# Four start addresses for the low weight buffers, one for all moving operands, and two instruction orders, in a one-core encoder kernel

## Chip, core and metric

The kernel runs on one core of a Trainium2 chip. The metric is the device time of one execution in microseconds (us); the table below gives the median of three runs. Each core has a matrix engine (PE, with its weight loads shown apart as PEld), a vector engine (DVE), a scalar engine (ACT), a general engine (POOL) and a queue that issues most transfers (SP).

## What is computed

Two layers over 272 tokens (16 learned meta tokens ahead of 256 others) of width 1024. Each layer is a parallel pair of token mixers (a chunked two-way retention with 8 heads, and a windowed attention with a sink) followed by an MLP with a squared ReLU. Cut to what matters:

```
h = concat([meta_tokens, x])                       # 272 x 1024
for l in range(2):
    u = rms_norm(h, norm_mix_pre[l])
    q_r, k_r, v_r, g_r, q_a, k_a, v_a, gate_r, gate_a = split(u @ w_in[l])
    y_r = retention_branch(q_r, k_r, v_r, g_r, log_decay) @ w_ret_o[l]
    y_a = attention_branch(q_a, k_a, v_a, attn_sink[l]) @ w_att_o[l]
    mix = (sigmoid(gate_r) * y_r + sigmoid(gate_a) * y_a) @ w_mix_o[l]
    h = h + rms_norm(mix, norm_mix_post[l])
    u = rms_norm(h, norm_ff_pre[l])
    h = h + rms_norm(square(relu(u @ w_ff1[l])) @ w_ff2[l], norm_ff_post[l])
return h[16:]
```

All of it is float32.

## The kernel before

**Products in three parts.** Each weight matrix is cut into units, 128 x 1024 numbers each, 130 per layer. A unit is fetched by one transfer into a `raw` buffer. ACT copies it, rounded, into a `wh` buffer (line 131), and DVE writes what the rounding lost, `raw - wh`, into a `wl` buffer (line 132). The tokens are split in the same way (`uh` and `ul`, `rh` and `rl`, `zh` and `zl`, `fh` and `fl`, two halves of `ao`). A product is then three matmuls, in `mm3`: high weights with high tokens (line 136), high weights with low tokens (line 137), low weights with high tokens (line 138). The weights are the stationary operand, which PE loads beforehand (PEld), 128 columns at a time; the tokens are the moving operand, 272 columns in layer 0, and 256 in most of layer 1, where the meta tokens are no longer needed (`c0 = 16`). A unit is eight such triples, 24 matmuls. The load for line 138, from `wl`, runs while line 137 streams; the loads for lines 136 and 137, both from `wh`, run while lines 138 and 136 stream. The last product of layer 1, `ff2t`, is turned round: the tokens (`fh`, `fl`) are stationary and 512 columns of `wh` or `wl` move (lines 848 to 850, 12 matmuls a unit).

**Where the buffers begin.** What matters here is the address of an operand within a partition, modulo 256 bytes; it is called its phase below. `raw`, `wh` and `wl` have rings of three, four and four buffers; unit i uses buffer i modulo 4, so DVE may be four units ahead of PE. All four `wh` and all four `wl` buffers begin at phase 0, and so does each 128-column piece of them (512 bytes). The slots of the tokens begin at phase 64, set by a small unused tile ("gap"), and a row of tokens is 320 numbers, 1280 bytes, so each row has the same phase. `tokens(..., at=n)` puts the tokens n columns into the row. With `at=32` the moving operand is at phase 192; in layer 1 `at=16` and `c0 = 16` give the same. So nearly all moving operands are at 192. The exceptions are `rl`, `zh` and `zl` of layer 0, at 0 (`at=48`); the 14 units of layer 1 that still need all 272 tokens, at 128; and in layer 1's MLP, the stationary `fh` and `fl`, at 64 (`at=48`), with `wh` and `wl` moving at 0.

**What sets the order.** A scheduler of the language orders the instructions of each engine; `tc.issue_after(x)` holds what is written in its block behind x. Each engine runs its own list in order. Three places are touched. In `value_r`, DVE scales a value head into `vt` (line 424), POOL copies its 16 meta tokens four times into `pads` (line 427, named `mine` in the code), and `centre()` gives PE one matmul from `pads` (line 430) and then two from `vt` (line 432), which show as two records each. In the retention, `meta(t)` forms scores of the meta tokens: PE (line 661), DVE `tmx` out of a bank of `ps_s` (through the helper of line 93), ACT `tm` (line 663), DVE `tm` (line 664). `similar` and `retained` are a head's scores (PE lines 680 and 681, DVE `sd`) and outputs (PE line 691 from `sd`, line 692 from `tm`). `ps_s` has two banks. At head 0, eight DVE steps `gt<-tg` add the tanh `tg` (ACT, line 647) to the gates `gt`.

Of the kernel before, what the change touches and what calls it, by code (L numbers as in the profile page):

```python
# [10 lines left out]
F32R = mybir.dt.float32r  # L11
# [6 lines left out]
P = 128  # L18
D = 1024
# [22 lines left out]
def encoder(ctx: ExitStack, tc: tile.TileContext, order, w, h_in, gains, dec, decm, sink, sinkm, tabs, mats, esel, masks, rel, relm, grow, out):  # L42
# [46 lines left out]
    def f(t):  # L89
        return t.bitcast(F32)  # L90

    def stt(o, a, s, b, op0=mul, op1=mul):
        V.scalar_tensor_tensor(out=o, in0=a, scalar=s, in1=b, op0=op0, op1=op1)
# [14 lines left out]
    def fetch(parts=1):  # L108
# [6 lines left out]
        for c in cuts:  # L115
            nc.sync.dma_start(raw[:, c], w[i][:, c])
            yield

    def unit(*name):
        i = len(order)  # L120
        order.append(name)
        if not raws:
            list(fetch())
        raw, cuts = raws.pop(0)
        wh = ring.tile([P, D], F32R, tag="wh", name="wh")
        wl = ring.tile([P, D], F32R, tag="wl", name="wl")
        for c in cuts:
            with ExitStack() as later:
                for ins in held.get(i, ()):
                    later.enter_context(tc.issue_after(ins))  # L130
                A.activation(wh[:, c], raw[:, c], AF.Copy)  # L131
                V.tensor_tensor(out=wl[:, c], in0=raw[:, c], in1=f(wh[:, c]), op=sub)  # L132
        return wh, wl
# [117 lines left out]
    def lead():  # L251
        x = [tokens(i, "u" + "hl"[i]) for i in range(2)]
        s8 = slot(7, "s8")
        ss = one.tile([P, T], F32, tag="ss", name="ss")
        ps = [bank("asas"[m], [T]) for m in range(4)]
        behind = {}

        def put(e, method, *args, **kw):
            if e in behind:
                with tc.issue_after(behind[e]):  # L260
                    ins = method(*args, **kw)
            else:
                ins = method(*args, **kw)
            behind[e] = ins.ins

        def squares(j):
            put("A", A.activation, s8[:, 2 * j:2 * j + 2], h[:, 2 * j:2 * j + 2], AF.Square)

        def add_squares(j):
            put("V", V.scalar_tensor_tensor, out=s8[:, 0:2], in0=s8[:, 0:2], scalar=4e-6 if j == 1 else 0.0, in1=s8[:, 2 * j:2 * j + 2], op0=add, op1=add)  # L270

        for k in range(KD):
            j, c = k // 2, slice(k % 2 * 512, k % 2 * 512 + 512)
            if k % 2 == 0:
                order.append(("lead", j))
                wh = ring.tile([P, D], F32R, tag="wh", name="wh")
                wl = ring.tile([P, D], F32R, tag="wl", name="wl")
            gk = g[:, 0, 0, k:k + 1]
            put("A", A.activation, wh[:, c], leads[j][:, c], AF.Copy)
            put("A", A.activation, x[0][:, k], h[:, k], AF.Copy, scale=gk)  # L280
            put("V", V.scalar_tensor_tensor, out=x[1][:, k], in0=h[:, k], scalar=gk, in1=f(x[0][:, k]), op0=mul, op1=sub)
            put("V", V.tensor_tensor, out=wl[:, c], in0=leads[j][:, c], in1=f(wh[:, c]), op=sub)
            if k in (3, 5, 7):
                squares((k - 3) // 2)
            if k in (6, 7):
                add_squares(k - 5)
            for m in range(4):
                o = k % 2 * 512 + m * P
                mm3(ps[m], wh[:, o:o + P], wl[:, o:o + P], x[0][:, k], x[1][:, k], k == 0, k == KD - 1)
        squares(3)  # L290
        add_squares(3)
        put("V", V.tensor_tensor, out=ss, in0=s8[:, 0], in1=s8[:, 1], op=add)
        held[len(order)] = [behind["V"]]
        return x, ss, ps
# [68 lines left out]
    for l in range(DEPTH):  # L363
# [52 lines left out]
        def value_r(hh):  # L416
            q, m = hh // 4, hh % 4
            if m == 0:
                tpv[q] = bank("s", [4, P]), [bank("t") for _ in range(2)]
            tpm, tps = tpv[q]  # L420
            vt = ready.get(hh)
            if vt is None:
                vt = two.tile([P, T], F32, tag="t1", name="vt")
                last = V.scalar_tensor_tensor(out=vt, in0=early.pop(0) if early else proj(u, 0, "a", "v_r", hh), scalar=-0.5, in1=rb, op0=mul, op1=mul)
                scaled.append(last.ins)
            mine = vtm[:, m]
            G.tensor_copy(mine[:, :, 16 * (m % 2):16 * (m % 2) + 16], fourfold(vt[:, 0:16]))

            def centre():
                PE.matmul(tpm[:, m], mine, mat["cen"], start=True, stop=True)  # L430
                for c in range(2):
                    PE.matmul(tps[c][:, m * P:(m + 1) * P], vt[:, 16 + c * P:16 + (c + 1) * P], mat["cen"], start=True, stop=True)
                if m == 3:
                    for c in range(2):
                        A.activation(vr[:, c, q * 512:(q + 1) * 512], tps[c], AF.Copy)
                    A.activation(vm[:, 4 * q:4 * q + 4], tpm, AF.Copy)
                    for r in odds:
                        low = vm[r, 4 * q:4 * q + 4]
                        V.tensor_tensor(out=low, in0=tpm[r], in1=f(low), op=sub)

            deferred.append(centre)
            if early:
                flush()
# [208 lines left out]
        def meta(t):  # L652
# [8 lines left out]
                PE.matmul(ps[:, c0:], kblk[min(i, 2)][:, t], q[:, c0:], start=i == 0, stop=i == 3)  # L661
            stt(x[:, c0:], ps[:, c0:], 0.125, x[:, c0:])
            A.activation(tm[:, t, c0:], x[:, c0:], AF.Copy)
            V.tensor_tensor(out=tm[lows, t, c0:], in0=x[lows, c0:], in1=f(tm[lows, t, c0:]), op=sub)

        sds, pos, pvs = {}, {}, {}

# [40 lines left out]
        similar(0)  # L708
        fill(F[3])
        with behind():  # L710
            meta(0)
        fill(F[4])
        for hh in range(8):
            with behind():
                if hh < 7:
                    similar(hh + 1)
                retained(hh)
            fill(F[7])
            if hh == 0:
                for m in range(KD):  # L720
                    stt(gt[:, m, c0:], tg[:, m, c0:], 1.0, gt[:, m, c0:], op0=add)
                rh, rl = tokens(7, "rh", at=32 - c0), tokens(8, "rl", at=(48, 16)[l])
            if hh % 2 and hh < 7:
                with behind():
                    meta((hh + 1) // 2)
            fill(F[6])
            with behind():
                last = normed(hh)
            fill(F[5])
# [16 lines left out]
                    mm3(ps[:, c0:], wh[:, sl], wl[:, sl], ao[:, 0, k, c0:], ao[:, 1, k, c0:], k == 0, k == 3)  # L746
                stt(tha[m][:, c0:], tha[m][:, c0:], 1.0, ps[:, c0:], op0=add)

        z = tokens(2, "zh", at=(48, 16)[l]), tokens(3, "zl", at=(48, 16)[l])
        for m in range(KD):  # L750
            ps = proj((rh, rl), c0, wide(), "ret_o", m)
            stt(thr[:, m, c0:], thr[:, m, c0:], 1.0, ps[:, c0:], op0=add)
# [25 lines left out]
        for m in range(KF):  # L778
            if m % KD == 0:
                a, b = ((5, 7), (8, 9), (6, 10), (2, 3))[m // KD]  # L780
                at = (32, 48)[l]
                low = [tokens(i, "fl", (4,), at) for i in ("10a", "10b")] if b == 10 else [tokens(b, "fl", at=at)]
                fs.append((rows(tokens(a, "fh", at=at)), sum(map(rows, low), [])))
            ps = proj(u, c0, wide(), "ff1", m)
            if l == 0 and 0 <= m - SUM < KD:
                accumulate(m - SUM)
# [201 lines left out]
```

## Time and profile before

| | |
|---|---|
| median of 3 runs | 874.17 us (872.90 to 877.86) |
| the profiled execution's own time | 876.77 us |
| its span, first to last instruction | 875.0 us |
| PE busy, PEld busy | 855.7 us (98%), 821.0 us (94%) |
| DVE, ACT, POOL busy | 604.0 us (69%), 558.1 us (64%), 55.4 us (6%) |
| DMA | 142 MB, mean 162 GB/s |

Times in the profile count from the first instruction of the span. A record of a matmul runs from its start to its modelled end and overlaps the next one, so its length is not what it costs; what it costs is the distance from its start to the start of the next. Where two rows of a timeline and the number of matmuls from one to the other are known, that distance is the difference over the number. A longer record goes with a longer distance: 276 ns with 113 ns, 281 ns with 118 ns.

### The profile page before, as it was taken

What the parts mean: (1) busy time and instruction counts of PE and PEld (TensorE: products, weight loads), DVE (VectorE), ACT (ScalarE), POOL (GpSimd) and SP (SyncE); (2) the same over time, 40 slices, a digit from 0 to 9 for tenths busy, and PEclk for the clock granted to TensorE, in tenths of its full rate; (3) what the DMA queues carried; (4) which work ended last, traced back from release to release, by engine and by line L of the source; (5) the groups of instructions that cost most, each with busy time, mean ns of one, the idle gap of its engine ahead of it and who ended that gap; (6) DMA issues with size and microseconds to landing.
All of it is one profiled execution on the core that took longest, in us unless ns stands there. A gap on an engine that the chain in (4) does not pass through costs nothing.

```text
span 875.0 us, 16673 instructions
## 1 busy us (share of the span) xinstructions
PE 855.7 (98%) x6514; PEld 821.0 (94%) x6514; DVE 604.0 (69%) x1113; ACT 558.1 (64%) x1034; POOL 55.4 (6%) x113
## 2 busy tenths in 40 slices
PE   9999999999999999999999999999999999999997
PEld 9899999999989999999989999999999999998885
DVE  7789788777768655544469898888686666554443
ACT  7447887666557877544355588976755588773432
POOL 2123320000000000000000032200000000000000
PEclk9999999999999999999999999999999999999999
DMA  8444444355645656656544535444366376656661
GB/s 300 161 142 123 122 143 129 118 166 157 179 147 163 197 171 177 184 171 183 178 121 145 155 119 162 143 148 121 121 199 205 104 216 210 195 199 192 181 187 67
DMA packets 41407, 142.15 MB, mean 162 GB/s; under 512 B 5360, under 2 KB 6256, under 8 KB 41328
## 3 DMA queue, kind: packets, MB, share of 16 engines
q1 hardware_dynamic: 40896, 140.43, 52.3%
q8 instruction: 51, 0.84, 0.4%
q10 hardware_dynamic: 432, 0.66, 0.2%
q14 instruction: 28, 0.23, 0.1%
HBM read 140.02 MB, written 1.05 MB: 161 GB/s over the span
## 4 chain that ended last, share of the span: by engine, by line
PE 79%; DVE 10%; ACT 7%; issue 2%; DMA 1%; POOL 0%; SPq 0%; DVEq 0%; ACTq 0%; POOLq 0%
PE ps_a L137 12%; PE ps_a L136 12%; PE ps_a L138 12%; PE ps_s L138 5%; PE ps_s L137 5%; PE ps_s L136 5%; PE ps_t L136 4%; PE ps_t L137 4%; PE ps_t L138 4%; DVE wl L132 3%; PE ps_a L850 2%; PE ps_s L850 2%; PE ps_s L848 2%; PE ps_a L848 2%; PE ps_a L849 2%
## 5 line engine op out<-in xcount | busy, mean ns | idle before, releaser
L132 DVE TENSOR_TENSOR wl<-raw,wh 128x1024 fp32r<-128x1024 f32 x256 | 312.7, 1224 | 204.9 <-ACT wh L131 203.1
L131 ACT ACTIVATE wh<-raw 128x1024 fp32r<-128x1024 f32 x256 | 270.0, 1058 | 205.4 <-PE ps_a L137 59.2
L136 PE MATMUL ps_a<-uh,wh 128*128 128x272 f32 (+1 forms) x912 | 265.6, 291 | 2.8 <-ACT uh L242 2.8
L137 PE MATMUL ps_a<-ul,wh 128*128 128x272 f32 (+1 forms) x912 | 259.5, 285 | 0.0
L138 PE MATMUL ps_a<-uh,wl 128*128 128x272 f32 (+1 forms) x912 | 259.2, 284 | 0.2 <-DVE wl L132 0.2
L136 PEld LDWEIGHTS ps_a<-uh,wh 128*128 128x128 f32 x912 | 172.4, 189 | 4.5 <-ACT uh L242 3.2
L137 PEld LDWEIGHTS ps_a<-ul,wh 128*128 128x128 f32 x912 | 172.5, 189 | 1.0
L138 PEld LDWEIGHTS ps_a<-uh,wl 128*128 128x128 f32 x912 | 172.2, 189 | 0.7 <-DVE wl L132 0.6
L138 PE MATMUL ps_s<-uh,wl 128*128 128x272 f32 (+1 forms) x184 | 52.1, 283 | 0.3 <-DVE wl L132 0.3
L136 PE MATMUL ps_s<-uh,wh 128*128 128x272 f32 (+1 forms) x184 | 52.1, 284 | 0.0
L137 PE MATMUL ps_s<-ul,wh 128*128 128x272 f32 (+1 forms) x184 | 52.1, 283 | 0.0
L136 PE MATMUL ps_t<-uh,wh 128*128 128x272 f32 (+1 forms) x152 | 43.2, 284 | 1.3 <-ACT uh L242 1.3
L137 PE MATMUL ps_t<-ul,wh 128*128 128x272 f32 (+1 forms) x152 | 43.1, 284 | 0.0
L138 PE MATMUL ps_t<-uh,wl 128*128 128x272 f32 (+1 forms) x152 | 42.8, 282 | 0.0
L138 PEld LDWEIGHTS ps_s<-uh,wl 128*128 128x128 f32 x184 | 34.6, 188 | 0.5 <-DVE wl L132 0.5
L136 PEld LDWEIGHTS ps_s<-uh,wh 128*128 128x128 f32 x184 | 34.9, 190 | 0.0
L137 PEld LDWEIGHTS ps_s<-ul,wh 128*128 128x128 f32 x184 | 34.8, 189 | 0.0
L136 PEld LDWEIGHTS ps_t<-uh,wh 128*128 128x128 f32 x152 | 28.6, 188 | 1.5 <-ACT uh L242 1.5
L137 PEld LDWEIGHTS ps_t<-ul,wh 128*128 128x128 f32 x152 | 28.6, 188 | 0.1
L138 PEld LDWEIGHTS ps_t<-uh,wl 128*128 128x128 f32 x152 | 28.6, 188 | 0.0
L97 DVE TENSOR_TENSOR fl<-ft,fh 128x272 fp32r<-128x272 f32 (+1 forms) x64 | 27.6, 433 | 1.0 <-ACT fh L96 0.9
L96 ACT ACTIVATE fh<-ft 128x272 fp32r<-128x272 f32 (+1 forms) x64 | 27.1, 424 | 1.7
(308 smaller groups left out, 1959.1 us busy)
## 6 DMA issues: line engine op xcount, KB each, us to landing
raw<-in_w SPq DMA_DIRECT2D x256, 512.0 KB, 3.6
leads<-in_w SPq DMA_DIRECT2D x6, 256.0 KB, 5.4
tab<-in_tabs SPq DMA_DIRECT2D x2, 544.0 KB, 6.1
h<-in_h_in SPq DMA_DIRECT2D x3, 272.0 KB, 5.4
out<-yt SPq DMA_DIRECT2D x3, 256.0 KB, 2.1
leads<-in_w ACTq DMA_DIRECT2D x2, 256.0 KB, 3.6
gj<-in_grow SPq DMA_DIRECT2D x1, 512.0 KB, 4.6
mats<-in_mats SPq DMA_DIRECT2D x1, 320.0 KB, 7.3
```

Source lines behind the costliest of these rows:

```text
L96: A.activation(xh, x, AF.Copy)
L97: V.tensor_tensor(out=xl, in0=x, in1=f(xh), op=sub)
L131: A.activation(wh[:, c], raw[:, c], AF.Copy)
L132: V.tensor_tensor(out=wl[:, c], in0=raw[:, c], in1=f(wh[:, c]), op=sub)
L136: PE.matmul(ps, ah, bh, start=first, stop=False)
L137: PE.matmul(ps, ah, bl, start=False, stop=False)
L138: return PE.matmul(ps, al, bh, start=False, stop=last)
L848: PE.matmul(pss[i], xh, wh[:, sl], start=kk == 0, stop=False)
L849: PE.matmul(pss[i], xh, wl[:, sl], start=False, stop=False)
L850: PE.matmul(pss[i], xl, wh[:, sl], start=False, stop=kk == KF - 1)
```

## The change

The four `wl` buffers get tags of their own and 16 more columns each (64 bytes), so that they begin at phases 0, 64, 128 and 192; unit i uses buffer i modulo 4 as before. Every `at` becomes `32 - c0`: the moving `rl`, `zh` and `zl` of layer 0 go from phase 0 to 192, and the stationary `fh` and `fl` of layer 1 from 64 to 192. Two orders are turned: in `centre()` the matmul from `pads` comes last; and the eight `gt<-tg` steps are held behind the last step of `meta(0)`.

```
+    def low_part(i):
+        return ring.tile([P, D + 16], F32R, tag=f"wl{i % 4}", name="wl", bufs=1)[:, :D]
...
-        wl = ring.tile([P, D], F32R, tag="wl", name="wl")
+        wl = low_part(i)
...
             def centre():
-                PE.matmul(tpm[:, m], mine, mat["cen"], start=True, stop=True)
                 for c in range(2):
                     PE.matmul(tps[c][:, m * P:(m + 1) * P], vt[:, 16 + c * P:16 + (c + 1) * P], mat["cen"], start=True, stop=True)
+                PE.matmul(tpm[:, m], mine, mat["cen"], start=True, stop=True)
...
-            V.tensor_tensor(out=tm[lows, t, c0:], in0=x[lows, c0:], in1=f(tm[lows, t, c0:]), op=sub)
+            return V.tensor_tensor(out=tm[lows, t, c0:], in0=x[lows, c0:], in1=f(tm[lows, t, c0:]), op=sub)
...
         with behind():
-            meta(0)
+            ready = meta(0)
...
                 for m in range(KD):
-                    stt(gt[:, m, c0:], tg[:, m, c0:], 1.0, gt[:, m, c0:], op0=add)
-                rh, rl = tokens(7, "rh", at=32 - c0), tokens(8, "rl", at=(48, 16)[l])
+                    with tc.issue_after(ready.ins):
+                        stt(gt[:, m, c0:], tg[:, m, c0:], 1.0, gt[:, m, c0:], op0=add)
+                rh, rl = tokens(7, "rh", at=32 - c0), tokens(8, "rl", at=32 - c0)
...
-        z = tokens(2, "zh", at=(48, 16)[l]), tokens(3, "zl", at=(48, 16)[l])
+        z = tokens(2, "zh", at=32 - c0), tokens(3, "zl", at=32 - c0)
...
-                at = (32, 48)[l]
-                low = [tokens(i, "fl", (4,), at) for i in ("10a", "10b")] if b == 10 else [tokens(b, "fl", at=at)]
-                fs.append((rows(tokens(a, "fh", at=at)), sum(map(rows, low), [])))
+                low = [tokens(i, "fl", (4,), 32 - c0) for i in ("10a", "10b")] if b == 10 else [tokens(b, "fl", at=32 - c0)]
+                fs.append((rows(tokens(a, "fh", at=32 - c0)), sum(map(rows, low), [])))
```

The scheduler answers to the two turned orders in the attention and retention stretches of both layers; outside them each engine's list is the same. Three places follow, first before, then after. After the change, line numbers below 116 are the same, later ones are 3 to 5 higher.

PE, in layer 0, where two value heads are centred at once, between the first matmuls of a unit. Before:

```order
L136 MATMUL ps_a<-uh,wh 128x272
L137 MATMUL ps_a<-ul,wh 128x272
L432 MATMUL ps_t<-mats,vt 128x128
L430 MATMUL ps_s<-mats,pads 128x128
L432 MATMUL ps_t<-mats,vt 128x128
L430 MATMUL ps_s<-mats,pads 128x128
L432 MATMUL ps_t<-mats,vt 128x128 x2
L138 MATMUL ps_a<-uh,wl 128x272
```

After:

```order
L139 MATMUL ps_a<-uh,wh 128x272
L140 MATMUL ps_a<-ul,wh 128x272
L434 MATMUL ps_t<-mats,vt 128x128 x2
L435 MATMUL ps_s<-mats,pads 128x128
L434 MATMUL ps_t<-mats,vt 128x128 x2
L435 MATMUL ps_s<-mats,pads 128x128
L141 MATMUL ps_a<-uh,wl 128x272
```

Each matmul from `pads` now stands behind both matmuls from its `vt`.

DVE, in layer 0, at the first attention keys and queries (`t` are temporaries of the rotation, `kal` the low part of the keys, `qa` the queries). Before:

```order
L451 TENSOR_TENSOR kal<-t_462,ka 64x272
L392 TENSOR_TENSOR t_510<-t_509,t_510 128x272
L451 TENSOR_TENSOR kal<-t_462,ka 64x272
L132 TENSOR_TENSOR wl<-raw,wh 128x1024
L93 SCALAR_TENSOR_TENSOR qa<-t_510,qa 64x272 x2
L424 SCALAR_TENSOR_TENSOR vt<-ps_a,rb 128x272
L132 TENSOR_TENSOR wl<-raw,wh 128x1024
```

After:

```order
L454 TENSOR_TENSOR kal<-t_462,ka 64x272
L394 TENSOR_TENSOR t_509<-ps_a,tab 128x272
L135 TENSOR_TENSOR wl<-raw,wh 128x1024
L454 TENSOR_TENSOR kal<-t_462,ka 64x272
L395 TENSOR_TENSOR t_510<-t_509,t_510 128x272
L427 SCALAR_TENSOR_TENSOR vt<-ps_a,rb 128x272
L135 TENSOR_TENSOR wl<-raw,wh 128x1024
L93 SCALAR_TENSOR_TENSOR qa<-t_510,qa 64x272 x2
```

The step that makes `vt` now stands ahead of the two `qa` steps, which stood ahead of it.

DVE, in layer 1, at the start of the retention. Before:

```order
L93 SCALAR_TENSOR_TENSOR sd<-ps_s,tt 128x256 x2
L93 SCALAR_TENSOR_TENSOR gt<-tg,gt 128x256 x5
L93 SCALAR_TENSOR_TENSOR tmx<-ps_s,tmx 128x256
L93 SCALAR_TENSOR_TENSOR gt<-tg,gt 128x256
L93 SCALAR_TENSOR_TENSOR thr<-ps_a,rb 128x256
L93 SCALAR_TENSOR_TENSOR sd<-ps_s,tt 128x256 x2
L664 TENSOR_TENSOR tm<-tmx,tm 64x256
L93 SCALAR_TENSOR_TENSOR gt<-tg,gt 128x256 x2
```

After:

```order
L93 SCALAR_TENSOR_TENSOR sd<-ps_s,tt 128x256 x2
L93 SCALAR_TENSOR_TENSOR tmx<-ps_s,tmx 128x256
L678 TENSOR_TENSOR tt<-tt,tb 128x128
L93 SCALAR_TENSOR_TENSOR thr<-ps_a,rb 128x256
L667 TENSOR_TENSOR tm<-tmx,tm 64x256
L93 SCALAR_TENSOR_TENSOR sd<-ps_s,tt 128x256 x2
L93 SCALAR_TENSOR_TENSOR gt<-tg,gt 128x256 x8
L135 TENSOR_TENSOR wl<-raw,wh 128x1024
```

`tmx` no longer stands behind five of the `gt` steps; all eight now stand in one block behind `tm`, with a `wl` step behind them. On PE the matmul from `tm` (line 692 before) moves from behind five matmuls of a unit to directly behind the two from `sd`.

## Rows read from the trace of the kernel before

**Rows 1.** The page: busy time, granted clock in 40 slices, chain by engine.

```profile
PE 855.7 (98%) x6514; PEld 821.0 (94%) x6514; DVE 604.0 (69%) x1113; ACT 558.1 (64%) x1034; POOL 55.4 (6%) x113
PEclk9999999999999999999999999999999999999999
PE 79%; DVE 10%; ACT 7%; issue 2%; DMA 1%; POOL 0%; SPq 0%; DVEq 0%; ACTq 0%; POOLq 0%
```

**Rows 2.** Timeline of PE, layer 0, `ff1`: start, length, instruction; 264 matmuls apart.

```profile
316.12 0.29 PE L136 MATMUL ps_a<-uh,wh 128*128 128x272 f32 x1
...
348.68 0.29 PE L136 MATMUL ps_s<-uh,wh 128*128 128x272 f32 x1
```

**Rows 3.** Timeline of PE, layer 0: `ret_o` (168 apart), then `mix` (120 apart).

```profile
205.85 0.28 PE L136 MATMUL ps_a<-rh,wh 128*128 128x272 f32 x1
...
226.75 0.29 PE L136 MATMUL ps_a<-rh,wh 128*128 128x272 f32 x1
...
235.76 0.29 PE L136 MATMUL ps_t<-zh,wh 128*128 128x272 f32 x1
...
250.80 0.29 PE L136 MATMUL ps_t<-zh,wh 128*128 128x272 f32 x1
```

**Rows 4.** Timeline of PE, layer 1: `ret_o` (192 apart), then `ff1` (624 apart).

```profile
638.88 0.28 PE L136 MATMUL ps_t<-rh,wh 128*128 128x256 f32 x1
...
661.49 0.28 PE L136 MATMUL ps_a<-zh,wh 128*128 128x256 f32 x1
...
700.81 0.28 PE L136 MATMUL ps_a<-uh,wh 128*128 128x256 f32 x1
...
771.53 0.28 PE L136 MATMUL ps_a<-uh,wh 128*128 128x256 f32 x1
```

**Rows 5.** Timeline of PE, layer 1, `ff2t`: 300 matmuls apart.

```profile
784.32 0.39 PE L848 MATMUL ps_s<-wh,fh 128*128 128x512 f32 x1
...
854.32 0.39 PE L848 MATMUL ps_s<-wh,fh 128*128 128x512 f32 x1
```

**Rows 6.** Groups of PE at 157.45, 172.34 and 142.55 us: count, busy us, mean ns.

```profile
L138 PE MATMUL ps_a<-uh,wl 128*128 128x272 f32 x1 | 0.3, 285 | 0.0
...
L138 PE MATMUL ps_a<-uh,wl 128*128 128x272 f32 x1 | 0.3, 292 | 0.0
...
L138 PE MATMUL ps_a<-uh,wl 128*128 128x272 f32 x1 | 0.3, 288 | 0.0
```

**Rows 7.** The same at 600.30 and 614.16 us, layer 1.

```profile
L138 PE MATMUL ps_a<-uh,wl 128*128 128x256 f32 x1 | 0.3, 276 | 0.0
...
L138 PE MATMUL ps_a<-uh,wl 128*128 128x256 f32 x1 | 0.3, 278 | 0.0
```

**Rows 8.** Timeline of PE in layer 0, with idle time before and what ended it.

```profile
28.59 0.49 PE L430 MATMUL ps_s<-mats,pads 128*128 128x128 f32 x2 [0.66 <-POOL pads L427]
...
43.60 0.49 PE L432 MATMUL ps_t<-mats,vt 128*128 128x128 f32 x2 [1.32 <-DVE vt L424]
44.82 0.80 PE L430 MATMUL ps_s<-mats,pads 128*128 128x128 f32 x2 [0.74 <-POOL pads L427]
```

**Rows 9.** Timeline of POOL and of DVE around the first of these.

```profile
27.37 1.17 POOL L427 COPY pads<-vt 128x64 f32<-128x64 f32 x1 [0.21 <-DVE vt L424]
...
27.23 1.22 DVE L132 TENSOR_TENSOR wl<-raw,wh 128x1024 fp32r<-128x1024 f32 x1
```

**Rows 10.** Timeline of DVE, ACT and PE in layer 1, start of the retention.

```profile
570.52 1.77 DVE L93 SCALAR_TENSOR_TENSOR gt<-tg,gt 128x256 f32<-128x256 f32 x5 [0.94 <-ACT tg L647]
...
575.32 2.35 DVE L132 TENSOR_TENSOR wl<-raw,wh 128x1024 fp32r<-128x1024 f32 x2
...
572.22 0.40 ACT L673 ACTIVATE tt<-rel,de 128x144 f32<-128x144 f16 x1
...
572.68 0.39 PE L680 MATMUL ps_s<-qk,qkl 128*128 128x256 f32 x1 [1.17 <-DVE tmx L93]
...
581.74 0.28 PE L138 MATMUL ps_a<-uh,wl 128*128 128x256 f32 x1
```

More of the change, by code (lines that the diff above doesn't have):

```diff
@@ L276, in lead @@
                 wh = ring.tile([P, D], F32R, tag="wh", name="wh")
-                wl = ring.tile([P, D], F32R, tag="wl", name="wl")
+                wl = low_part(j)
             gk = g[:, 0, 0, k:k + 1]
```

## The prediction, made before the changed kernel had run

> **What bounds the kernel now.** I read the page first: PE is busy for 98% of the span, PE makes up 79% of the chain that ended last, DVE 10% and ACT 7%, and the granted clock is at its upper level, 2.4 GHz, in all 40 slices [rows 1]. So a change pays or costs mainly through the distance from one matmul's start to the next. This I take from the timeline. In layer 0's `ff1`, 264 matmuls of 272 columns take 32.56 us, 123.33 ns each [rows 2]; 272 cycles of 2.4 GHz would be 113.3 ns, so some 10 ns of each is something else. Nothing waits there, and only addresses differ between this stretch and others of the same shape. `mix` of layer 0, all of whose moving operands are at phase 0, takes 15.04 us for 120, 125.33 ns; `ret_o` of layer 0, where only `rl` is at 0, 20.90 us for 168, 124.40 ns [rows 3]. Phases therefore matter, by a nanosecond or three. In layer 1, 256 columns take 113.33 ns in `ff1` (70.72 us for 624) but 117.76 ns in `ret_o` (22.61 us for 192), with the same phases, moving at 192 and weights at 0 [rows 4]: there are two rhythms at this width, and the trace does not say what picks one. `ff2t` takes 70.00 us for 300, 233.33 ns [rows 5].
>
> **The low weights' phases.** What changes is the load from `wl`, which runs while line 137 streams: 1824 of the 5472 loads for `mm3`. Of them 1040 are in layer 0 (130 units of 8), 672 in the 256-column units of layer 1, and 112 in its 272-column units, whose moving operand is at 128. A quarter of the buffers stays at phase 0. For the other phases the retention gives a price, because the key blocks that PE loads behind line 138 step through all four phases from head pair to head pair (a key row is 1088 bytes, 64 modulo 256). The last matmul of a unit ahead of such a load, moving at 192, has a record of 285 ns when the key is at 0, 292 ns when at 64, 288 ns when at 192 [rows 6], and the row at 128 reads the same as the last. Against the first that is 0, 7, 3 and 3 ns, 3.25 on average. In a stretch without interruption records swing by about 3 ns from one matmul to the next, and 285 is the low one, so against the mean of the swing it is 0, 5.5, 1.5 and 1.5, or 2.1. I take 2.5. `ret_o` supports a net cost of this size: there one matmul of three has moving and stationary operand at the same phase, as buffer 3 will have, and a triple takes 3 x 1.07 = 3.2 ns more than in `ff1` [rows 2, 3]. Layer 0: 1040 x 2.5 ns = 2.6 us. At 256 columns the record reads 276 ns at phase 0 and 278 ns at 64 [rows 7]; I let the other two cost nothing: 672 x 2 ns / 4 = 0.3 us. The 112 triples with a moving operand at 128 I leave at 0. **Sum +2.9 us**, on the path, since nothing covers PE. Upper end: 7 ns for three buffers of four in all triples, 1824 x 5.25 ns = 9.6 us. Lower end: no row shows a phase that is faster than 0, but layer 1's best rhythm is 113.33 / 256 = 0.443 ns a column, at which 272 would take 120.4; 2.9 ns off 780 loads is -2.3 us.
>
> The Trainium skill speaks against any price here: "SBUF — State Buffer", section "Who interferes with whom", gives PE two independent read ports, one for the moving operand and one for the weight loads, and says that PE never waits on anyone. By it this term would be 0. The records of 285 and 292 ns with the same moving operand and different weights [rows 6] disagree, as far as single matmuls can, and so do the 125.33 ns of `mix` [rows 3].
>
> **The moving operands.** `mix` of layer 0 goes from 125.33 to 123.33 ns (192 matmuls, 0.38 us) and `ret_o` from 124.40 to 123.33 (192, 0.21 us): **-0.6 us** [rows 2, 3]. In `ff2t` the stationary tokens go from 64 to 192, so that the moving `wh` stands 64 ahead of them instead of 192, and `wl` anything from 0 to 192. No row has 512 columns with another distance. The nearest is the distance of 64 at 272 columns (key at 128 under 192), +3 ns in its record; with the same 2.5 ns for all 384 matmuls I take **+1.0 us**. Ends: 7 ns, +2.7 us, and the rate of 0.443 ns a column, 226.7 instead of 233.33 ns, -2.5 us.
>
> **The turned orders.** (a) At 28.59 us PE waits 0.66 us for the copy to `pads` [rows 8]. That copy takes 1.17 us beside a `wl` step of 1.22 us that starts 0.14 us ahead of it [rows 9]. After the change that `wl` step stands behind another `vt` step and two steps on `tab`, and one more pair of matmuls from `vt` stands ahead of the waiting one: -0.6. (b) At 43.60 PE waits 1.32 us for a `vt` [rows 8]; it is moved ahead of two `qa` steps, of some 0.35 us each by the like steps on `gt` (1.77 us for five [rows 10]): -0.7. (c) The wait of 0.74 us at 44.82 [rows 8] stays, for `wl` still follows `vt` at once; only a pair of `vt` matmuls more covers it, -0.2. (d) In layer 1, PE's second score matmul waits 1.17 us for `tmx` to free a bank, because five `gt` steps stand ahead of it that wait for the tanh; these start at 570.52 [rows 10]. That wait goes. Next late is `tm`: ACT has two steps ahead of it, the second ends at 572.62 [rows 10]; with 0.40 us on ACT and some 0.4 on DVE, `tm` is there at 573.4. PE would come to it at about 572.5 (572.68 less 1.17, and 1.0 for the scores and the two matmuls from `sd`), so some 0.9 of the 1.17 comes back: -0.3. Layer 0 has a smaller wait of the same kind; -0.2. Queued behind the block of eight `gt` steps (2.8 us) is a `wl` step, which moves from 575.32 to about 577; what it writes is first read at 581.74 [rows 10], so it stays covered, and if the cover were gone it would cost up to 1.7 us. SP's list is unchanged; POOL's copies go in the same order. **Sum -2.0 us.** Ends: all these waits go, -4.2; or one as long as the longest here, 1.3, comes new where the scheduler shuffled the softmax steps, +1.3 on top of nothing gained.
>
> **The sum.** 2.9 + 1.0 - 0.6 - 2.0 = +1.3 us. On the profiled execution's own 876.77 us (span 875.0 and 1.77 around it) that is 878.1; that execution lies 2.6 us above the median of the runs, 874.17, and the change carried to the median gives **875.5 us**.
>
> **Rivals.** (1) The phases of the weights cost nothing, as the section on ports would have it: the orders and layer 0's moving operands alone, -2.6 us, 871.6. For it: the prices rest on single matmuls beside interruptions. Against: `ret_o` and `mix`. (2) Slower: the rhythm at 256 columns. Layer 1's `uh` units run mostly in the 113.33 ns rhythm, `ret_o` and `mix` in that of 117.76 [rows 4]. If three differing phases of four knock the 512 triples on `uh` out of the fast one, that is 1536 x 4.43 ns = 6.8 us more, 882.3. It decides from about half of them on (3.1 us more than the forecast reaches +0.5%). For it: the rhythm breaks without any change of phase; against: a key at 64 lengthens a record by only 2 ns there [rows 7], and after many interruptions the fast one came back. (3) Faster: no price on the phases and all waits gone, -4.2 - 0.6, 869.4; or one of the new distances is at the best rate a column. Against: `tm` takes the place of `tmx`.
>
> **How the numbers follow.** Forecast 0.52, (1) 0.16, (2) 0.20, (3) 0.12. 0.5%, about what a measurement of this kernel can tell from no change, is 4.4 us: 869.8 and 878.5. Faster: (3) and a little of (1), 0.13. Slower: (2) and the upper tail of the forecast, 0.23. Same: 0.64. The range leaves out the outermost of (2) and (3): 870.5 to 882.
>
> **What would show it.** In the changed trace: layer 0's `ff1` near 124.2 ns a matmul, with the surplus in line 140 (137 before) and in three units of four, most with the buffer at 64; `mix` of layer 0 like `ff1`; `ff2t` at 235 to 237 ns; layer 1's `ff1` records at 276 to 277 ns, not 281; no wait of PE for `tmx`, one of under 1 us for `tm`; the waits for `pads` near 28 us gone. The prediction is wrong in its main step if units of the four buffers take the same time, or if one at a new phase is faster than at 0; and wrong in sign if layer 1 settles in the slow rhythm.

## The result, and the profile after

The changed kernel takes **879.35 us** (median of 10 runs, 878.77 to 881.80) against 874.13 us (10 runs, 872.56 to 877.86) of the kernel before: a ratio of **1.0058, interval 1.0045 to 1.0072**, or 5.1 us slower. The forecast was 875.5 us, the range 870.5 to 882.0. The time lies in the range, 3.9 us above the forecast and just past the 0.5% at which "slower" begins; the prediction gave 0.64 to "same" and 0.23 to "slower". The profiled execution took 879.07 us (span 877.3). That of before lay 2.6 us above its own median, so the two traces differ by only 2.3 us in span.

The page after, busy time and chain by engine, answers to [rows 1]: PE is busy 4.7 us longer for the same 6514 instructions, and has 83% of the chain instead of 79%.

```profile
PE 860.4 (98%) x6514; PEld 826.7 (94%) x6514; DVE 603.4 (69%) x1113; ACT 559.6 (64%) x1034; POOL 50.1 (6%) x113
...
PE 83%; DVE 9%; ACT 5%; issue 1%; DMA 1%; POOL 0%; SPq 0%; DVEq 0%; ACTq 0%; POOLq 0%
```

Where it goes is seen by setting the start of the same unit side by side in both timelines of PE (us):

| first matmul of | before | after | difference |
|---|---|---|---|
| unit 20, after the value heads of layer 0 | 87.54 | 84.13 | -3.4 |
| `ff1` of layer 0 | 258.81 | 256.22 | -2.6 |
| layer 1 | 454.32 | 455.02 | +0.7 |
| `ff2t` of layer 1 | 778.64 | 781.91 | +3.3 |
| the last unit | 862.72 | 865.12 | +2.4 |

The first 85 us gain, the stretches of `mm3` behind them lose, and `ff2t` gains.

Not all of the gain at the start is the change's. Behind the two waits near 44 us [rows 8] the granted clock of the kernel before fell to its lower level, 1.2 GHz, for some 3.4 us; behind the like waits of the change it did not. The digits of [rows 1] hide this, for a 9 stands for anything from 90% up. The same stretch by windows (start:end, length, PE busy with its matmuls, granted clock, share and GB/s of DMA), before and after:

```profile
44.80:48.00 3.20, 3.18 (x14) 0.50 0.65 202
```

```profile
44.80:48.00 3.20, 3.20 (x28) 1.00 0.25 65
```

Half the matmuls fit into it. The clock fell there in all three traces with the old order of `centre()` and in three of the eleven with the new one. The price shows in two runs below with the same instruction lists: from the matmul behind the second wait to unit 12 the orders alone, whose clock fell, took 9.61 us, orders and tokens together, whose clock stayed up, 8.05. So about 1.6 of the 3.4 us are the clock of these two executions. How often it falls in executions without a trace is not known.

Timeline of PE after (start, length, instruction), layer 0's `ff2`: the first matmuls of five units in a row, with `wl` at 128, 192, 0 and 64, and of one 20 units later.

```profile
365.62 0.29 PE L139 MATMUL ps_a<-fh,wh 128*128 128x272 f32 x1
...
368.60 0.29 PE L139 MATMUL ps_a<-fh,wh 128*128 128x272 f32 x1
...
371.61 0.29 PE L139 MATMUL ps_a<-fh,wh 128*128 128x272 f32 x1
...
374.65 0.29 PE L139 MATMUL ps_a<-fh,wh 128*128 128x272 f32 x1
...
377.68 0.29 PE L139 MATMUL ps_t<-fh,wh 128*128 128x272 f32 x1
...
437.98 0.29 PE L139 MATMUL ps_s<-fh,wh 128*128 128x272 f32 x1
```

The units take 2.98, 3.01, 3.04 and 3.03 us; before, each took 24 x 123.33 ns = 2.96 [rows 2]. The slowest is the one whose `wl` is still at 0. Over the 576 matmuls from the first row to the last it is 72.36 us, 125.6 ns each.

The same view of layer 1: `ret_o` (192 matmuls apart), `ff1` (624), `ff2t` (300).

```profile
639.96 0.28 PE L139 MATMUL ps_t<-rh,wh 128*128 128x256 f32 x1
...
662.43 0.28 PE L139 MATMUL ps_a<-zh,wh 128*128 128x256 f32 x1
...
701.72 0.28 PE L139 MATMUL ps_a<-uh,wh 128*128 128x256 f32 x1
...
774.67 0.29 PE L139 MATMUL ps_a<-uh,wh 128*128 128x256 f32 x1
...
787.52 0.40 PE L851 MATMUL ps_s<-wh,fh 128*128 128x512 f32 x1
...
856.80 0.39 PE L851 MATMUL ps_s<-wh,fh 128*128 128x512 f32 x1
```

`ret_o` is at 117.0 ns (117.76 before), `ff1` at 116.9 (113.33 before [rows 4]), `ff2t` at 230.9 (233.33 before [rows 5]).

The turned orders, in the timeline with idle time and its releaser, beside [rows 8] and [rows 10]: the wait for `pads` near 28 us is gone, that for `vt` is 0.56 us instead of 1.32, that for `pads` behind it 0.98 instead of 0.74; and in layer 1 PE waits 0.54 us for `tm` where it waited 1.17 for `tmx`.

```profile
41.05 0.71 PE L434 MATMUL ps_t<-mats,vt 128*128 128x128 f32 x4 [0.56 <-DVE vt L427]
42.74 0.49 PE L435 MATMUL ps_s<-mats,pads 128*128 128x128 f32 x2 [0.98 <-POOL pads L430]
...
574.38 0.39 PE L695 MATMUL ps_o<-tm,vm 128*128 128x256 f32 x1 [0.54 <-DVE tm L667]
```

### The profile page after: what moved, and what is told of

It is laid out like the page before. It is cut to its first block, busy times and chain, and to the rows that moved or that the text cites. A ratio compares the mean times of both kernels' runs of the same rounds, so it can differ in the third digit from the quotient of the medians.

```text
span 877.3 us, 16670 instructions
## 1 busy us (share of the span) xinstructions
PE 860.4 (98%) x6514; PEld 826.7 (94%) x6514; DVE 603.4 (69%) x1113; ACT 559.6 (64%) x1034; POOL 50.1 (6%) x113
## 4 chain that ended last, share of the span: by engine, by line
PE 83%; DVE 9%; ACT 5%; issue 1%; DMA 1%; POOL 0%; SPq 0%; DVEq 0%; ACTq 0%; POOLq 0%
PE ps_a L141 13%; PE ps_a L140 13%; PE ps_a L139 13%; PE ps_s L141 5%; PE ps_s L140 5%; PE ps_s L139 5%; PE ps_t L139 4%; PE ps_t L140 4%; PE ps_t L141 4%; DVE wl L135 3%; PE ps_s L852 2%; PE ps_a L851 2%; PE ps_s L851 2%; PE ps_a L853 2%; PE ps_a L852 2%; PE ps_s L853 2%
```

## Experiments: one part at a time

All ratios are against the kernel before, on the same chip in the same session; the sessions were on several chips, so kernels of different sessions are compared by their ratios. Rates are those of one traced execution of each kernel. "Rate" is the mean distance from matmul to matmul, worked out from two rows of PE's timeline as above.

**The orders alone.** Edit: the hunks on `centre()`, `meta` and `gt` of the change, nothing else.

> Only the two turned orders; all addresses as in the kernel before. In the trace of the whole change, layer 0's ff1 begins 2.4 us earlier than before although the units ahead of it run slower, so the orders must give more than 2.4 us there. Theory (the orders work as forecast or better): -2.5 to -4 us, no wait of PE for pads near 28 us and none for tmx in layer 1, and the distance from matmul to matmul in ff1 stays at 123.33 ns in layer 0 and 113.33 in layer 1. Rival (the orders give nothing, and the earlier start is a gift of the new addresses): within 0.5 us of the kernel before.

Measured: ratio 0.9983 (0.9964 to 1.0002), -1.5 us, with an end just above zero. In the trace PE is 2.4 us ahead of before at layer 0's `ff1` and 2.1 ahead at the end; the clock fell near 44 us in both traces. The rates are those of before, 123.33 and 113.33 ns. In layer 1's attention, PE's timeline with idle time shows a wait for `pn` (first row; the second is that of before, which is gone); in the table of waits (us in total, times, longest) `tmx` no longer appears, and `tm` is in its place:

```profile
529.33 0.44 PE L603 MATMUL ps_t<-mats,pn 128*128 128x128 f32 x2 [0.48 <-ACT pn L596]
```

```profile
510.00 0.44 PE L603 MATMUL ps_t<-mats,pn 128*128 128x128 f32 x2 [0.94 <-ACT pn L596]
```

```profile
PE ps_o L692 <- DVE tm L664: 0.8, 1, 0.8
```

The orders work in layer 0. In layer 1 they gain 0.3 us at `tm` and lose 0.5 before it, in the attention, where the scheduler has put the softmax steps in another order. The theory holds in kind, and its -2.5 lies inside the interval; the interval alone does not exclude the rival (within 0.5 us), the trace does, with 1.4 us gained across the unit whose wait for `pads` went.

**The four low buffers alone.** Edit: `low_part` and its two uses.

> Only the four start addresses of the wl buffers; orders and moving operands as in the kernel before. Theory (the whole loss of the change comes from here, and it is a slower rhythm of all matmuls of a unit, not a surcharge on one matmul in three): layer 0's ff1 at 125.6 ns a matmul instead of 123.33, layer 1's ff1 at 117.0 instead of 113.33; over 1040 and 512 triples that is 7.1 and 5.6 us, less what the attention stretches hide, so +7 to +12 us. Rival (the forecast's own price, 2.5 ns for one matmul in three): +2 to +4 us, and ff1 near 124.2 and 113.9 ns. ff2t gets its wl from all four phases here and its tokens stay at 64: if its gain of 2.5 ns a matmul comes from the wl phases it shows here, if it comes from the tokens it does not.

Measured: 1.0090 (1.0066 to 1.0115), **+7.9 us**. The timeline, layer 0's `ff2` (576 apart) and layer 1's `ff1` (624):

```profile
369.26 0.29 PE L139 MATMUL ps_a<-fh,wh 128*128 128x272 f32 x1
...
441.62 0.29 PE L139 MATMUL ps_s<-fh,wh 128*128 128x272 f32 x1
...
706.24 0.28 PE L139 MATMUL ps_a<-uh,wh 128*128 128x256 f32 x1
...
779.30 0.29 PE L139 MATMUL ps_a<-uh,wh 128*128 128x256 f32 x1
```

That is 125.6 and 117.1 ns; 300 matmuls of `ff2t` take 69.74 us, 232.5 ns. The whole loss comes from here; the forecast's price of 2.9 us lies outside the interval. `ff2t` is 0.9 ns faster than before, so most of its gain in the change is not from the buffers.

**The tokens alone.** Edit: the hunks with `at=32 - c0`.

> Only the tokens: rl, zh and zl of layer 0 and the stationary fh and fl of layer 1 go to phase 192; wl at 0 and the orders as before. Theory: ret_o and mix of layer 0 run at 123.3 ns like ff1 (-0.6 us), and ff2t at 230 ns instead of 233.3 (-1.3 us): -1.5 to -2 us in all. Rival 1 (the forecast's price for ff2t): ff2t at 236 ns, +0.4 us in all. Rival 2 (the distance between moving and stationary phase has no part in it): within 0.3 us, and ret_o and mix stay at 124.4 and 125.3 ns.

Measured: 0.9987 (0.9970 to 1.0004), -1.1 us. Timeline: layer 0's `ret_o` (192 apart), layer 1's `ff1` (624), `ff2t` (300).

```profile
205.42 0.28 PE L136 MATMUL ps_a<-rh,wh 128*128 128x272 f32 x1
...
229.10 0.28 PE L136 MATMUL ps_t<-zh,wh 128*128 128x272 f32 x1
...
699.88 0.28 PE L136 MATMUL ps_a<-uh,wh 128*128 128x256 f32 x1
...
773.38 0.28 PE L136 MATMUL ps_a<-uh,wh 128*128 128x256 f32 x1
...
786.29 0.39 PE L847 MATMUL ps_s<-wh,fh 128*128 128x512 f32 x1
...
854.95 0.39 PE L847 MATMUL ps_s<-wh,fh 128*128 128x512 f32 x1
```

`ret_o` is at 123.33 ns as forecast, and `ff2t` at 228.9: -4.4 ns for 384 matmuls, -1.7 us, where the forecast had +1.0. The middle pair was not expected by anyone: `ff1` of layer 1, whose operands on PE this kernel does not move, ran at 117.8 ns instead of 113.33, 2.8 us longer. With `wl` at 0 that stretch has two rhythms, and addresses alone do not set which one an execution gets: the next kernel has all addresses of this one, and ran it at 113.3.

**Orders and tokens, `wl` at 0.** Edit: the change without `low_part`.

> The change without its four wl addresses: turned orders and tokens at 192, wl at 0. Theory (the parts add up): the sum of the two runs with the orders alone and the tokens alone, -4 to -5.5 us, about 869 us, and faster than both kernels. Rival (the parts meet: with the waits gone, the units run on without the pauses in which the rhythm is regained, or another wait comes last): less than the larger of the two alone.

Measured: 870.56 us, **0.9942** (0.9919 to 0.9964), -5.1 us, faster than both kernels. The three alone add up to the change, -1.5 - 1.1 + 7.9 = +5.3 against +5.1. But orders and tokens together give -5.1, where alone they add up to -2.6, and the buffers on top of them then cost 10.2 instead of 7.9. With intervals of about 2 us to either side of each, whether the parts meet stays open.

## Experiments: what a start address costs

**All four `wl` buffers at one phase, or at two.** Edit, cut from `low_part`, with x = 16, 32 or 48 for phase 64, 128 or 192; the tile behind restores what follows:

```
+        if i == 0:
+            ring.tile([P, x], F32, name="pre", bufs=1)
         wl = ring.tile([P, D], F32R, tag="wl", name="wl")
+        if i == 0:
+            ring.tile([P, 64 - x], F32, name="post", bufs=1)
```

and for 0, 128, 0, 128 `low_part` with `D + 32` in place of `D + 16`.

> All four wl buffers at phase 64; tokens at 192 and orders as in the change. In the changed kernel a steady cycle of four units in layer 0's ff1 takes 3.04, 3.02, 2.99 and 3.01 us for wl at 0, 64, 128 and 192, 2.96 for each before. Theory (what costs is the change of the phase from unit to unit: it breaks a rhythm, so that even the units at 0 pay): 123.33 ns a matmul in layer 0's ff1, as with all at 0, and a time near that of the kernel with all at 0, 870.6 us, up to 3 us more where layer 1's ff1 falls into the slow rhythm. Rival (each phase has its own price, and the unit behind it pays a part): 3.02 us a unit, 125.8 ns; over the 64 units of layer 0's MLP alone +3.8 us, and layer 1's ff1 at 118 ns, +3 us: about 878.

> All four wl buffers at phase 128. In layer 1 of the changed kernel the units with wl at 128 are the only ones near the fast rhythm (2.75 us, 114.6 ns; the others 2.82 to 2.83, 118). Theory (change alone costs): layer 0's ff1 at 123.33 ns, layer 1 as with all at 0: ret_o and mix at 117.8, ff1 at 113.3 or 118. Rival (each phase has its own price): layer 0's ff1 at 124.6 ns, +1.9 us over its MLP; all of layer 1 in the fast rhythm, ret_o and mix too (113.4 ns instead of 117.8; 20 units of 24, -2.1 us), so about 870 us, and little scatter between executions.

> All four wl buffers at phase 192, that of the moving tokens. Theory (change alone costs): layer 0's ff1 at 123.33 ns, about 870.6 to 874 us. Rival (each phase has its own price): 3.01 us a unit, 125.4 ns, +3.2 us over layer 0's MLP, layer 1's ff1 at 118 ns: about 877. ff2t, where wh moves at 0 over tokens at 192: 230 ns with wl at 0; in the changed kernel units with wl at 192 take most there (2.80 us against 2.76), so 233 by the rival.

> wl buffers at 0, 128, 0, 128. Theory (change alone costs): layer 0's ff1 well above 123.33 ns in the units at 0 and at 128 alike, about 125.6 as in the changed kernel, and layer 1's ff1 in the slow rhythm: 877 to 879 us. Rival (each phase has its own price): units at 0 as with all at 0 (2.96 us), units at 128 at 2.99; about 871 to 873 us.

Measured (rates in ns; layer 0 is `ff2`; tokens at 192 and orders turned throughout):

| `wl` at | ratio (interval) | us | layer 0 | L1 `ret_o` | L1 `ff1` | `ff2t` |
|---|---|---|---|---|---|---|
| 0 | 0.9942 (0.9919 to 0.9964) | -5.1 | 123.33 | 117.8 | 113.3 | 228.9 |
| 64 | 1.0125 (1.0107 to 1.0144) | +10.9 | 126.67 | 118.2 | 118.2 | 232.2 |
| 128 | 0.9989 (0.9974 to 1.0003) | -1.0 | 125.56 | 113.3 | 113.3 | 230.4 |
| 192 | 1.0107 (1.0084 to 1.0130) | +9.4 | 125.56 | 122.2 | 117.8 | 233.3 |
| 0, 128, 0, 128 | 0.9969 (0.9957 to 0.9980) | -2.7 | 123.89 | 113.3 | 113.3 | 230.2 |
| 0, 64, 128, 192 (the change) | 1.0058 (1.0045 to 1.0072) | +5.1 | 125.6 | 117.0 | 116.9 | 230.9 |

My theory, that a change of phase from unit to unit is what costs, falls: the worst kernel of all has one phase throughout. The rival stands in the main: each phase has its own price, and it depends on the number of columns. But the price depends on the neighbours too, so the rival's numbers, read from units in the order of four, were too low. A unit at 128 takes 125.56 ns a matmul with all at 128, but 124.4 in the order of four and in the alternating kernel; one at 64 takes 126.67 with all at 64, but 126.0 in the order of four. At 256 columns the alternating kernel runs `ret_o` at 113.3 in its units at 0 as well. Rows of that kernel, layer 0's `ff2`, a unit at 0 (2.96 us) and one at 128 (2.99):

```profile
351.01 0.28 PE L139 MATMUL ps_s<-fh,wh 128*128 128x272 f32 x1
...
353.97 0.28 PE L139 MATMUL ps_s<-fh,wh 128*128 128x272 f32 x1
...
356.96 0.28 PE L139 MATMUL ps_s<-fh,wh 128*128 128x272 f32 x1
```

Rows for 64 (layer 0's `ff2`, 576 apart), then for 128 (the same, and layer 1's `ret_o`, 192 apart):

```profile
368.52 0.29 PE L144 MATMUL ps_a<-fh,wh 128*128 128x272 f32 x1
...
441.48 0.29 PE L144 MATMUL ps_s<-fh,wh 128*128 128x272 f32 x1
```

```profile
366.13 0.29 PE L144 MATMUL ps_a<-fh,wh 128*128 128x272 f32 x1
...
438.45 0.29 PE L144 MATMUL ps_s<-fh,wh 128*128 128x272 f32 x1
...
639.55 0.28 PE L144 MATMUL ps_t<-rh,wh 128*128 128x256 f32 x1
...
661.31 0.28 PE L144 MATMUL ps_a<-zh,wh 128*128 128x256 f32 x1
```

At 64 the groups by line of that stretch (count, then busy us and mean ns of a record) show where the price lies: the matmul from `wl` itself has a record of 293 ns, the one ahead of it, beside whose stream the load from `wl` runs, 289, the third 287. With all at 0 the same groups read 287, 286 and 286, so the price falls on the first two.

```profile
L146 PE MATMUL ps_a<-fh,wl 128*128 128x272 f32 x96 | 28.1, 293 | 0.0
L145 PE MATMUL ps_a<-fl,wh 128*128 128x272 f32 x96 | 27.7, 289 | 0.0
L144 PE MATMUL ps_a<-fh,wh 128*128 128x272 f32 x96 | 27.6, 287 | 0.0
```

**Is it the phase or the distance?** Edit: every `at` 16 more (64 bytes), and the "gap" tile 64 instead of 48 numbers, which moves all weight buffers by 64 bytes too. (This tile stands ahead of the weight rings, behind the slots of the tokens: it sets where the weights begin, and not, as was said ahead of the prediction, where the slots do. The temporaries behind the rings move by 64 bytes as well, which the expectation does not say; the MLP stages read here multiply tokens and weights alone.)

> All tokens 64 bytes further on (phase 192 to 0, and 128 to 192) and all weight buffers, wh and wl, 64 bytes further on (0 to 64), so that each distance between a moving and a stationary operand is as in the kernel with the orders turned and wl at 0; small operands keep theirs. Theory (only the distance counts): the same times, 123.33 ns in layer 0's ff1, ret_o and mix, 228.89 in ff2t, about 870.6 us. Rival (the phase itself counts, of the one or the other): 125.3 to 126.7 ns as with tokens at 0 or wl at 64, 875 to 885 us.

Measured: 872.08 us, 0.9958 (0.9938 to 0.9978), whose interval overlaps that of the kernel with `wl` at 0. Layer 0's `ff2` (576 apart), its `ff1` (192 apart), and `ff2t` (300):

```profile
362.89 0.29 PE L136 MATMUL ps_a<-fh,wh 128*128 128x272 f32 x1
...
433.93 0.29 PE L136 MATMUL ps_s<-fh,wh 128*128 128x272 f32 x1
...
266.67 0.29 PE L136 MATMUL ps_s<-uh,wh 128*128 128x272 f32 x1
...
290.99 0.29 PE L136 MATMUL ps_a<-uh,wh 128*128 128x272 f32 x1
...
779.14 0.39 PE L848 MATMUL ps_s<-wh,fh 128*128 128x512 f32 x1
...
847.81 0.39 PE L848 MATMUL ps_s<-wh,fh 128*128 128x512 f32 x1
```

`ff2` runs at 123.33 ns and `ff2t` at 228.9, to the digit as with the same distances elsewhere, though `wl` is at 64: at these two widths the distance counts, not the phase. At 256 columns this is less clear: `ret_o` of layer 1 ran at 113.33 ns here, and at 117.78 in all four traces with the same distances at the old addresses. The middle pair, 24.32 us for 192, 126.67 ns, shows that 272 columns too have a second rhythm; this execution left it after 12 units, behind a single matmul of another kind (line 183, at 306.19).

A rival is left untested. `wl` moved against `wh` in every one of these kernels, as well as against the tokens, and this run keeps both distances. That the distance to the tokens matters is shown by the run of the tokens alone (`mix` at 123.33 instead of 125.33 ns, with all weights in place); which of the two distances sets the price of `wl` is not shown.

**The unit at 0 in the order of four.** Edit: `D + (48, 16)[i % 2]` in `low_part`, so that buffers begin at 0, 192, 0, 192.

> wl buffers at 0, 192, 0, 192; the rest as in the change. In the changed kernel the units at 0, which come behind units at 192, take 126.67 ns a matmul in layer 0's ff2, though all at 0 take 123.33 and though units at 0 between units at 128 take 123.33 too. Theory (a unit at 0 pays for what it inherits from one at 192): units at 0 at 126.7, units at 192 at 125.5 or less. Rival (the whole order of four makes it): units at 0 at 123.33, units at 192 at about 125.6.

A single execution (878.00 us, which without an interval says little). Layer 0's `ff2`, the units with `wl` at 0, 192, 0, 192:

```profile
364.39 0.29 PE L139 MATMUL ps_a<-fh,wh 128*128 128x272 f32 x1
...
367.35 0.29 PE L139 MATMUL ps_a<-fh,wh 128*128 128x272 f32 x1
...
370.36 0.29 PE L139 MATMUL ps_a<-fh,wh 128*128 128x272 f32 x1
...
373.33 0.28 PE L139 MATMUL ps_a<-fh,wh 128*128 128x272 f32 x1
...
376.33 0.29 PE L139 MATMUL ps_t<-fh,wh 128*128 128x272 f32 x1
```

2.96, 3.01, 2.97 and 3.00 us: a unit at 0 behind one at 192 pays next to nothing. The theory of an inheritance from 192 falls. In the order of four the unit at 0 takes 3.04 us, which is just what a unit takes in the second rhythm of the run before (126.67 ns): it looks as if the units at 0 were in that rhythm. In the change's `ff1` the first whole unit at 0 behind an inserted matmul still took 2.965 us (from 311.37), the next ones 3.04. What puts them there stays open.

**A phase for each width.** If prices go by width, layer 0 and `ff2t` want 0 and the rest of layer 1 wants 128.

> Turned orders and tokens at 192 as in the change; wl at 0 in layer 0 and under ff2t, at 128 in the rest of layer 1. Theory (each phase has its own price at each width: at 272 columns 123.33 ns with wl at 0 and 125.56 at 128, at 256 columns 117.78 or 113.33 at 0 and always 113.33 at 128, at 512 columns 228.89 at 0 and 230.39 at 128): layer 0 as with all at 0, ret_o and mix of layer 1 at 113.33 ns, 2 us less there, ff1 of layer 1 never in the slow rhythm, ff2t at 228.89: 867.5 to 869 us, faster than with all at 0 (870.56) and faster than both kernels. Rival (what a run of units inherits decides, and the switch from 0 to 128 or back breaks it): ret_o and mix stay at 117.78, or ff2t above 230, and 870 to 872 us.

This kernel did not do what its expectation says. Its buffers were 128 bytes wider, and so themselves began at 0, 128, 0, 128; the units of both layers alternated. It took 871.38 us, 0.9949 (0.9930 to 0.9969), and its layer 0 ran at 123.9 ns like the kernel that alternates. So it says nothing on the theory. Mended:

```
+    def low_part(i):
+        late = int(UNITS <= i < 2 * UNITS - 32)
+        at = 32 * (late ^ i % 2)
+        return ring.tile([P, D + 32], F32R, tag=f"wl{i % 4}", name="wl", bufs=1)[:, at:at + D]
```

> Turned orders and tokens at 192; wl at 0 in layer 0 and under ff2t, at 128 in the rest of layer 1. (The attempt before it at the same thing had buffers 128 bytes wider, which themselves begin at 0, 128, 0, 128, so that its units alternated in both layers.) Theory (each phase has its own price at each width): layer 0 at 123.33 ns as with all at 0, ret_o, mix and ff1 of layer 1 at 113.33 ns, ff2t at 228.89; against the kernel with wl at 0 everywhere 2 us less in ret_o and mix, and no slow ff1: 867.5 to 869.5 us, the fastest here. Rival (the switch from 0 to 128 breaks a rhythm): ret_o and mix at 117.78 or ff2t above 230 ns, 870 to 872 us. Costs that stay under both: the units of layer 1 with 272 columns, now with wl at 128 under tokens at 128, some 0.1 us each where they pay, 14 of them.

Measured: **869.10 us, 0.9927** (0.9908 to 0.9945), -6.4 us, runs from 868.42 to 870.97. Layer 1's `ret_o` (192 apart) and `ff1` (624):

```profile
636.47 0.28 PE L141 MATMUL ps_t<-rh,wh 128*128 128x256 f32 x1
...
658.23 0.28 PE L141 MATMUL ps_a<-zh,wh 128*128 128x256 f32 x1
...
696.73 0.28 PE L141 MATMUL ps_a<-uh,wh 128*128 128x256 f32 x1
...
767.45 0.28 PE L141 MATMUL ps_a<-uh,wh 128*128 128x256 f32 x1
```

113.33 ns in both; 300 matmuls of `ff2t` take 68.67 us, 228.9 ns: each stage has the rate that its distance gave elsewhere. It beats both kernels; against the kernel with `wl` at 0 everywhere the two intervals overlap, and only the trace, with `ret_o` and `mix` 1.7 us shorter, says that it is better. (The clock fell near 44 us in this trace and not in that one, so only stages are compared.)

## Why the prediction was right or wrong

**What bounds the kernel** was read rightly in the main: the distance from matmul to matmul and a few waits decided the time. One reading was wrong: the clock was not at its upper level throughout, as the windows from 44.8 to 48.0 us show, and the 1.6 us that this cost were not in every execution.

**The low weights' phases: the step that failed, by size.** The forecast was +2.9 us; the buffers alone cost 7.9 us (5.8 to 10.1), and the trace of the change against that of the kernel without them shows 8.5 us: 1.6 up to layer 0's `ff1`, 3.3 in its MLP, 2.9 in layer 1 and 0.7 in `ff2t`. For buffers that all have one phase the order was read rightly from [rows 6]: 64 worst, 128 and 192 alike. In the change itself it was not: the prediction calls its main step wrong if a unit at a new phase is faster than one at 0, and in layer 0's `ff2` all three are (2.98, 3.01 and 3.03 us against 3.04). The size was wrong too. I took 2.5 ns for each load from `wl`, with 0 for the quarter at phase 0. The uniform kernels give for a triple 3 x (126.67 - 123.33) = 10 ns at 64 and 6.7 at 128 and 192, 5.8 on average; in the order of four it is 3 x 2.3 = 6.9. Three mistakes lie in it. A record beside an interruption shows one matmul, while the price falls on its neighbour too (293 and 289 ns above, for 287 and 286). The full readings of 0, 7, 3 and 3, 3.25 on average, I then took down to 2.5 for a swing of the records, which made it worse. And the unit at phase 0 was taken to be free, where in this order it is the slowest (3.04 us). My upper end of 9.6 us, 5.25 ns for each triple, was too low per triple in layer 0's MLP; over both layers without `ff2t` it held, at 7.8 us.

**Layer 1: rival 2, in the main.** I let 256 columns cost 0.3 us on a difference of 2 ns between two records [rows 7], and gave 0.20 to the rival that the 113.33 ns rhythm breaks. It broke: `ff1` ran at 116.9 ns, three units of four near 118, and layer 1 lost 2.9 us between its start and `ff2t`. That is less than the rival's 6.8, since it priced all `uh` triples and since the buffer at 128 has the fast rhythm of its own, which even sped `ret_o` up from 117.76 to 117.0. The run with the tokens alone sets a limit to this reading: `ff1` can fall into 117.8 ns with every address that PE reads there as before.

**The moving operands.** `mix` and `ret_o` of layer 0: -0.6 us forecast; the run of the tokens alone has exactly this (PE gains 0.6 us from the start of `ret_o` to the start of `ff1`). In the change it is eaten by the buffers: `mix` is at 125.3 ns. **`ff2t` had the wrong sign**: +1.0 forecast, and -1.7 us from the tokens, of which the buffers take 0.7 back. What failed here is the transfer of a price from 272 columns, with tokens moving, to 512, with weights moving. The other end of that term, -2.5 us, was nearer.

**The turned orders.** -2.0 forecast; -1.5 (-3.1 to +0.2) by the runs of the orders alone, -2.1 by their trace. By steps: (a) came, and more with it: PE gains 1.4 us across that unit in every trace with the turned orders, where 0.6 was forecast. (b) came only in part: the wait for `vt`, 1.32 us before, is anything from 0.4 to 1.6 us in the eleven traces with the new order (0.56 in the change, 0.9 in the orders alone, 1.5 in the last experiment), so it is not the order alone that sets it. (c) had the wrong sign, 0.98 us for 0.74. What the prediction did not have is the clock that may fall behind these two waits. (d) came to the digit: `tm` took the place of `tmx`, with 0.8 us for 1.17 where the buffers are as before, and PE gains 0.36 us there, forecast -0.3. What the forecast had only among its ends, a wait from the shuffled softmax steps, came in small: the one for `pn` of 0.94 us went, and two came, 0.59 us for `ex` and 0.48 for `pn`; across the unit with the latter PE loses 0.7 us.

**Rival 1**, no price on the weights' phases, is refuted. The Trainium skill ("SBUF — State Buffer", section "Who interferes with whom") has PE read moving operand and weights through two independent ports. By it the term would be 0. In the runs only the start of `wl` differs between 123.33 and 126.67 ns, so the measurement decides against it; what the two reads share, the runs don't show. **Rival 3**, a gain, needed the phases to be free; without the four buffers its kind of time came (870.56 us).

**What would show it.** Right: no wait for `tmx`, one below 1 us for `tm`, none for `pads` near 28 us, `mix` like `ff1`. Wrong: 124.2 ns in layer 0's `ff1` (125.6), the surplus in line 140 alone (spread over the lines), most with the buffer at 64 (with that at 0), 235 to 237 ns in `ff2t` (230.9), records of 276 ns in layer 1 (280 in the mean). That the time lies in the range is in part luck, since the errors have both signs: +2.3 in layer 0's buffers, +2.6 in layer 1's, -2.0 in `ff2t`, between -0.1 and +0.5 in the orders: +2.8 to +3.4 of the 3.9 us that were missed.

## What to carry to other kernels

In a kernel that TensorE bounds, the start of the weight buffers relative to the moving operand, modulo 256 bytes, can be a tuning parameter: here 1.8% lay between the best and the worst of four phases. Set it for each width by measuring a whole stage at each of the four distances, all buffers alike. A mix has to be measured as a mix: in layer 0 the order of four ran a little slower than the mean of its four (125.6 against 125.3 ns), 0 and 128 in turn faster than the mean of theirs (123.89 against 124.4). Don't read such a price from a record at the edge of an interruption, nor carry it from one width to another. And before two traces are compared at their starts, look at the granted clock by windows of a few microseconds. When buffers are widened to move what they hold, recompute where each of them begins.

## What the runs showed of the hardware

- Distance from the stationary `wl` to the moving operand (moving minus stationary, modulo 256; `wh` at distance 192, so that its distance to `wl` changes along), all four buffers alike, one traced execution of each of the other distances and several of 192: at 272 columns 192 is best (123.33 ns), then 64 and 0 (125.56), then 128 (126.67). At 256 columns, in `ret_o` and `ff1` of layer 1, 64 gave 113.33 in each stage, 192 gave 113.33 or 117.8, 128 gave 118.2, 0 gave 117.8 to 122.2. At 512, with weights moving over tokens and `wh` at distance 64, `wl` at 64 gave 228.9, at 192 230.4, at 128 232.2, at 0 233.3.
- There are two rhythms: layer 1's `ff1`, the same instructions at the same addresses, ran at 113.33 ns in one execution (orders and tokens) and at 117.8 in another (the tokens alone), 2.8 us apart. Layer 0's `ff1` changed from 126.67 to 123.33 ns within one execution, behind one matmul of another kind. What picks the rhythm was not found, and how much of the scatter between executions is due to it (7 us in the kernel before) was not measured.
- The granted clock fell from 2.4 to 1.2 GHz for some 3.4 us near 44 us in six of fourteen traces, at a cost of about 1.6 us. Ahead of it PE had waited 0.9 to 1.6 us for `vt` and 0.7 to 1.0 for `pads`; in the eight traces in which it stayed up the first wait was 0.4 to 1.4 us and the second 1.0. So the length of the first alone does not decide it.
